# Making the low part of a weight block on GpSimd in four instructions of 256 columns in place of one of 1024

## The chip, the cores and the metric

The kernel runs on one core of one Trainium2 chip. The metric is the device time of one execution in microseconds (us), the median of several runs. TensorE is called PE in the profile, VectorE DVE, ScalarE ACT and GpSimd POOL.

## The reference

A two-layer network on 512 tokens of width 1024, all in float32. Layer 0 mixes tokens with a state-space block (`mamba2_mixer`), layer 1 with windowed attention. Both then run `peer_ffn`, a feed-forward part that picks experts, and `ple_add`, a gated addition. Cut to the part in which most of the time is spent:

```python
def peer_ffn(x, norm_g, q_w, sub_keys, u, v):
    h = rmsnorm(x, norm_g).reshape(T, D)
    q = (h @ q_w).reshape(T, PEER_HEADS, 2, PEER_HALF)
    s = jnp.einsum('thcd,ckd->thck', q, sub_keys)
    s1, i1 = lax.top_k(s[:, :, 0], PEER_TOPK)
    s2, i2 = lax.top_k(s[:, :, 1], PEER_TOPK)
    ...
    best_s, best_pos = lax.top_k(cand_s, PEER_TOPK)
    idx = jnp.take_along_axis(cand_i, best_pos, axis=-1)
    gate = jax.nn.softmax(best_s, axis=-1)
    a = jnp.einsum('nd,nhkd->nhk', hb, u[ib])
    w = gb * jax.nn.gelu(a, approximate=False)
    return jnp.einsum('nhk,nhkd->nd', w, v[ib])
```

The 16384 experts have a row in `u` and a row in `v`, each of 1024 numbers.

## The kernel before

**Products in three terms.** Each float32 operand of a large product is split into a high part (rounded to the type that TensorE takes fast) and a low part, the rest. `mm3` adds high by high, high weight by low data, and low weight by high data (lines L199, L200, L201). A weight block is 128 rows by 1024 columns and holds eight 128x128 tiles; a product over a block is 24 matmuls, three for each tile `k`.

**The split of a weight block.** `next_w` hands out the blocks in a fixed order. A block is loaded by a DMA into `wraw` (three buffers), ACT copies it into `whi` (L168), and then `lo_eng` writes `wlo = wraw - whi` (L169), one instruction of 1024 columns. `lo_eng` is GpSimd everywhere but in the loop over the `v` blocks, where it is DVE. The split runs two blocks ahead of the product that uses it (`SA = 2`). 391 blocks are split on GpSimd, 256 on DVE.

**The stages.** The state-space block, the query products, the gates and the attention work on 512 tokens. In `peer`, the first 128 tokens are done by gathering rows: GpSimd issues an indirect DMA for a row of `u` for each token (`row`, L692), DVE multiplies it with the token's vector, which lies in PSUM (`pair`, L675). The other 384 tokens are done densely: a loop over the 128 blocks of `u` ("the u loop"), then a loop over the 128 blocks of `v` ("the v loop"). Between the blocks of the u loop DVE works off a list of items (`bg`): the top-k search (L781 to L785, `cand` L800), the decoding of the positions (`eq` L828 to L838, `gk` L847), and for four tokens at a time a pair of one-hot tables, `early` (L877) and `og` (L879), which PE multiplies (`gmm`, L892). How many items come after a block is set by a credit (`BRATE`), and how many gathers by `URATE`.

**Order.** Nothing reorders the program: each engine runs its instructions in the order of the code, and semaphores make them wait. On GpSimd a gather therefore stands between two splits, and on PE a `gmm` between two blocks.

Of the kernel before, what the change touches and what calls it, by code (L numbers as in the profile page):

```python
# [11 lines left out]
F32 = _mybir.dt.float32  # L12
# [5 lines left out]
OP = _mybir.AluOpType  # L18
# [4 lines left out]
D = 1024  # L23
# [6 lines left out]
ND = NT - NG  # L30
NJ = HEADS * TOPK
LAG = 4
PAIR = (5, 6)
QT = 4
GSCALE = 32768.0
# [26 lines left out]
class Net:  # L62
    def __init__(self, ctx, tc, t):
# [3 lines left out]
        for i in range(8):  # L67
            if i not in PAIR:
                self.bank(i)
# [25 lines left out]
    def bank(self, i):  # L95
        return (self.psp if i in PAIR else self.psum).tile([P, 512], F32, name=f"bank{i}")

# [55 lines left out]
    def next_w(self):  # L153
        if self.wn is not None:
            w, self.wn = self.wn, None
            return w
        nc = self.nc
        i = self.nuse
        while self.ndma < min(len(self.srcs), i + self.LA + 1) or self.nsplit < min(len(self.srcs), i + self.SA + 1):
            if self.ndma < min(len(self.srcs), i + self.LA + 1) and self.ndma < self.nsplit + 3:  # L160
                self.ahead()
                continue
            if self.nsplit >= min(len(self.srcs), i + self.SA + 1):
                break
            r = self.split_q.pop(self.nsplit)
            hi = self.hl.tile([P, D], F32R, name="whi")
            lo = self.hl.tile([P, D], F32R, name="wlo")
            nc.scalar.activation(hi, r, AF.Copy)  # L168
            self.lo_eng.tensor_tensor(lo, r, hi.bitcast(F32), op=OP.subtract)  # L169
            self.split_q["w", self.nsplit] = (hi, lo)  # L170
            self.nsplit += 1
        self.nuse += 1
        return self.split_q.pop(("w", i))
# [463 lines left out]
    def peer(self, L):  # L637
# [28 lines left out]
        def gather_step():  # L666
            i = self.gi
            if i is None or i >= 2 * NJ + LAG:
                return
            self.gi += 1  # L670
            if i >= LAG:
                c, r = i - LAG, got.pop(i - LAG)
                j = c % NJ
                if c < NJ:
                    vt.scalar_tensor_tensor(r, r, 1.0, self.pair, op0=OP.mult, op1=OP.mult,  # L675
                                            accum_out=wg[:, 0, j:j + 1])
                    if j % 16 == 15:
                        js = slice(j - 15, j + 1)
                        vt.tensor_scalar(wg[:, 0, js], wg[:, 0, js], rv0, None, op0=OP.mult)
                        nc.scalar.activation(wg[:, 1, js], wg[:, 0, js], AF.Gelu)  # L680
                elif j == 0:
                    vt.tensor_scalar(yg, r, wg[:, 0, j:j + 1], None, op0=OP.mult)
                else:
                    vt.scalar_tensor_tensor(yg, r, wg[:, 0, j:j + 1], yg, op0=OP.mult, op1=OP.add)  # L684
            c = i - LAG - 8
            if c >= 0 and c % 16 == 15 and c < NJ:
                js = slice(c - 15, c + 1)
                vt.tensor_tensor(wg[:, 0, js], wg[:, 1, js], gate[:, js], op=OP.mult)
            if i < 2 * NJ:
                got[i] = rowt[i % len(rowt)]  # L690
                j = i % NJ
                nc.gpsimd.indirect_dma_start(  # L692
                    out=got[i], out_offset=None, in_=t["u"] if i < NJ else t["v"].rearrange("a p d -> (a p) d"),
                    in_offset=bass.IndirectOffsetOnAxis(ap=eg[:, j:j + 1], axis=0))
# [21 lines left out]
        def load_ga(j):  # L716
            if j < NBLK:
                gal[j] = gsz[0][:, j % 4, :ND]
                nc.sync.dma_start(gal[j], GA[j])
# [24 lines left out]
        with ExitStack() as ctx:  # L744
# [231 lines left out]
            for j in range(NBLK):  # L976
# [19 lines left out]
                if j >= NBLK - 3:  # L996
                    load_ga(j - NBLK + 3)
            while self.gi < NJ + LAG:
                gather_step()
        with vctx:  # L1000
# [6 lines left out]
            for j in range(NBLK):  # L1007
# [4 lines left out]
                if j == NBLK - VT:  # L1012
                    while self.gi < 2 * NJ + LAG:
                        gather_step()
# [536 lines left out]
```

## Time and profile before

| | |
|---|---|
| median of 3 runs | 3542.51 us (3539.78 to 3543.81) |
| profiled execution | 3534.58 us, of it 3532.8 us from the first to the last instruction |
| busy PE | 3377.5 us (96%) |
| busy DVE | 2808.9 us (80%) |
| busy GpSimd | 1676.7 us (47%) |
| busy ACT | 1453.3 us (41%) |

Busy time counts an instruction from its start to its end. If an instruction is held up after its start, that time is in it too, so a busy engine need not be a working one. PE is near full, and what a change can give is what PE stands idle. The u loops lie at about 650 to 1330 us (layer 0) and 2250 to 2930 us (layer 1).

### The profile page before, as it was taken

The numbers are of one execution on the slowest core, as the hardware profiler recorded it, in microseconds if no ns is written. First come the engines' busy times: TensorE is split into PE (matmuls) and PEld (weight loads), VectorE is DVE, ScalarE is ACT, GpSimd is POOL, SyncE is SP. The second block draws the span as 40 slices with busy tenths as digits, with TensorE's granted clock in tenths as the row PEclk, the third lists the DMA queues.
The fourth block names the chain that finished last, engine by engine and source line by source line (L and its number), as shares of the span: only waits on it lengthen the run. The fifth ranks groups of instructions, "written<-read, shape, count | busy, mean of one in ns | idle before, by whom it ended". The sixth has DMA issues, their size and how long they took to land.

```text
span 3532.8 us, 50923 instructions
## 1 busy us (share of the span) xinstructions
PE 3377.5 (96%) x18814; PEld 3107.8 (88%) x18814; DVE 2808.9 (80%) x4878; ACT 1453.3 (41%) x2198; POOL 1676.7 (47%) x995
## 2 busy tenths in 40 slices
PE   8999999989999999999998899989999999999997
PEld 5777777988999999999996667979999999999996
DVE  7677776899999857877777865899999848877775
ACT  4333333434444533333334553434444543333334
POOL 3333344566776684322215225566676685322213
PEclk9999999999999999999999999999999999999999
DMA  3222222478888899999983112478887899999992
GB/s 115 90 72 72 72 66 62 152 252 294 286 310 273 303 330 360 361 336 344 338 283 103 42 64 86 128 243 310 282 306 265 309 323 354 362 345 333 343 311 87
DMA packets 357290, 827.42 MB, mean 234 GB/s; under 512 B 30000, under 2 KB 196528, under 8 KB 350896
## 3 DMA queue, kind: packets, MB, share of 16 engines
q1 hardware_dynamic: 235136, 448.59, 39.6%
q0 software_dynamic: 73728, 268.47, 21.1%
q10 hardware_dynamic: 48176, 107.10, 7.8%
q8 instruction: 147, 2.41, 0.3%
q14 instruction: 103, 0.84, 0.1%
HBM read 717.09 MB, written 106.95 MB: 233 GB/s over the span
## 4 chain that ended last, share of the span: by engine, by line
PE 64%; DVE 27%; issue 4%; DMA 2%; POOL 2%; ACT 2%; DVEq 0%; SPq 0%; POOLq 0%; ACTq 0%
PE bank L199 19%; PE bank L200 19%; PE bank L201 19%; DVE row L675 4%; PE bank L892 3%; DVE og L879 3%; DVE early L877 2%; DVE eq L835 2%; DVE cand L800 1%; DVE eq L832 1%; POOL wlo L169 1%; POOL row L692 1%; PE bank L539 1%; DVE cu L483 1%; DMA gsz<-GA 1%
## 5 line engine op out<-in xcount | busy, mean ns | idle before, releaser
L169 POOL TENSOR_TENSOR wlo<-wraw,whi 128x1024 fp32r<-128x1024 f32 x391 | 966.9, 2475 | 850.0 <-ACT whi L168 803.5
L168 ACT ACTIVATE whi<-wraw 128x1024 fp32r<-128x1024 f32 x647 | 685.2, 1061 | 700.8 <-issue 329.9
L201 PE MATMUL bank<-hhi,wlo 128*128 128x384 f32 x2048 | 697.8, 341 | 19.9 <-POOL wlo L169 19.7
L199 PE MATMUL bank<-hhi,whi 128*128 128x384 f32 x2048 | 708.6, 346 | 0.0
L200 PE MATMUL bank<-hlo,whi 128*128 128x384 f32 x2048 | 696.3, 340 | 0.0
L200 PE MATMUL bank<-vlo,whi 128*128 128x384 f32 x2032 | 684.4, 337 | 2.9 <-DVE vlo L741 2.9
L199 PE MATMUL bank<-vhi,whi 128*128 128x384 f32 x2032 | 685.0, 337 | 0.2 <-ACT vhi L739 0.2
L201 PE MATMUL bank<-vhi,wlo 128*128 128x384 f32 x2032 | 683.8, 337 | 0.0
L692 POOL DMA_INDIRECT row<-v,eg x256 | 317.5, 1240 | 718.7 <-DVE yg L684 704.2
L169 DVE TENSOR_TENSOR wlo<-wraw,whi 128x1024 fp32r<-128x1024 f32 x256 | 313.4, 1224 | 152.7 <-ACT whi L168 151.8
L201 PEld LDWEIGHTS bank<-hhi,wlo 128*128 128x128 f32 x2048 | 388.2, 190 | 24.7 <-POOL wlo L169 24.6
L199 PEld LDWEIGHTS bank<-hhi,whi 128*128 128x128 f32 x2048 | 390.9, 191 | 0.0
L200 PEld LDWEIGHTS bank<-hlo,whi 128*128 128x128 f32 x2048 | 389.6, 190 | 0.0
L200 PEld LDWEIGHTS bank<-vlo,whi 128*128 128x128 f32 x2032 | 383.0, 188 | 4.8 <-DVE vlo L741 4.8
L199 PEld LDWEIGHTS bank<-vhi,whi 128*128 128x128 f32 x2032 | 383.0, 188 | 1.0 <-ACT vhi L739 0.5
L201 PEld LDWEIGHTS bank<-vhi,wlo 128*128 128x128 f32 x2032 | 383.0, 188 | 0.0
L675 DVE SCALAR_TENSOR_TENSOR row<-row,pair 128x1024 f32<-128x1024 f32 x256 | 305.4, 1213 | 70.3 <-DMA row<-u,eg 70.3
L684 DVE SCALAR_TENSOR_TENSOR yg<-row,wg,yg 128x1024 f32<-128x1024 f32 x254 | 348.6, 1372 | 13.8 <-DMA row<-v,eg 13.7
L987 ACT ACTIVATE ga<-bank 128x384 f32<-128x384 f32 x256 | 125.7, 491 | 514.2 <-PE bank L201 513.9
L692 POOL DMA_INDIRECT row<-u,eg x256 | 282.9, 1105 | 98.0 <-DVE row L675 48.7
L199 PE MATMUL bank<-z,whi 128*128 128x512 f32 x728 | 322.6, 443 | 6.2 <-DVE sg L1131 6.2
L200 PE MATMUL bank<-z,whi 128*128 128x512 f32 x728 | 292.1, 401 | 3.4 <-DVE z L259 3.4
(321 smaller groups left out, 5151.6 us busy)
## 6 DMA issues: line engine op xcount, KB each, us to landing
wraw<-ut SPq DMA_DIRECT2D x256, 512.0 KB, 4.6
wraw<-v SPq DMA_DIRECT2D x256, 512.0 KB, 6.1
wraw<-wlin SPq DMA_DIRECT2D x135, 512.0 KB, 3.5
GA<-ga ACTq DMA_DIRECT2D x256, 192.0 KB, 4.5
G<-gsz ACTq DMA_DIRECT2D x48, 1024.0 KB, 7.3
gv<-G SPq DMA_DIRECT2D x96, 512.0 KB, 9.5
gsz<-GA SPq DMA_DIRECT2D x256, 192.0 KB, 7.2
PJ<-nf ACTq DMA_DIRECT2D x16, 256.0 KB, 2.0
```

What stands on the lines that cost most here:

```text
L168: nc.scalar.activation(hi, r, AF.Copy)
L169: self.lo_eng.tensor_tensor(lo, r, hi.bitcast(F32), op=OP.subtract)
L199: mm(out, whi, xhi, start=start, stop=False)
L200: mm(out, whi, xlo, start=False, stop=False)
L201: mm(out, wlo, xhi, start=False, stop=stop)
L675: vt.scalar_tensor_tensor(r, r, 1.0, self.pair, op0=OP.mult, op1=OP.mult, accum_out=wg[:, 0, j:j + 1])
L684: vt.scalar_tensor_tensor(yg, r, wg[:, 0, j:j + 1], yg, op0=OP.mult, op1=OP.add)
L692: nc.gpsimd.indirect_dma_start(out=got[i], out_offset=None, in_=t["u"] if i < NJ else t["v"].rearrange("a p d -> (a p) d"), in_offset=bass ...
L835: vt.tensor_tensor(eq[:, :n], eq[:, :n], eq[:, n:2 * n], op=OP.add)
L879: vt.tensor_tensor(og, o[:, 0:1].to_broadcast([P, 2, P, QT]), gT[:, :, None, ts].to_broadcast([P, 2, P, QT]), op=OP.mult)
L892: mm(ps[:, q * P:(q + 1) * P], o[0][:, 1, :, q], o[1][:, j, :, q], start=(j == 0), stop=(j == 1))
L987: nc.scalar.activation(ga[:, NG:], ps[:, NG:], AF.Gelu)
```

## The change

The instruction on L169 is replaced by a loop. On GpSimd it writes 256 columns four times; on DVE it stays one of 1024 columns. Lines behind it move by up to three.

```diff
+LOP = 4
...
             nc.scalar.activation(hi, r, AF.Copy)
-            self.lo_eng.tensor_tensor(lo, r, hi.bitcast(F32), op=OP.subtract)
+            n = D if self.lo_eng is nc.vector else D // LOP
+            for q in range(0, D, n):
+                self.lo_eng.tensor_tensor(lo[:, q:q + n], r[:, q:q + n], hi.bitcast(F32)[:, q:q + n], op=OP.subtract)
```

GpSimd's queue in the u loop before (a `DMA` row is a gather; names in brackets are the semaphores that the row waits for):

```order
152 L692 DMA row_5517<-u,eg 128x1024 [waits DMASW3_49,DVE_49]
153 L169 TENSOR_TENSOR wlo<-wraw,whi 128x1024 [waits DMAHW4_49,PE_49,Activation_49]
154 L692 DMA row_5518<-u,eg 128x1024 [waits DMASW4_49,DVE_49]
155 L692 DMA row_5519<-u,eg 128x1024 [waits DMASW5_49,DVE_49]
156 L169 TENSOR_TENSOR wlo<-wraw,whi 128x1024 [waits DMAHW6_49,PE_49,Activation_49]
```

The same place in GpSimd's queue after the change:

```order
251 L695 DMA row_4687<-u,eg 128x1024 [waits DMASW2_49,DVE_49]
252 L172 TENSOR_TENSOR wlo<-wraw,whi 128x256 [waits DMAHW2_49,PE_49,Activation_49]
253 L172 TENSOR_TENSOR wlo<-wraw,whi 128x256 x3
254 L695 DMA row_5772<-u,eg 128x1024 [waits DMASW3_49,DVE_49]
```

Only the first of the four waits; the other three follow it at once, and the gathers stay where they were.

PE's queue at the start of a block of the u loop before (`hhi` and `hlo` are the two parts of the data):

```order
3737 L199 MATMUL bank_7464<-hhi_4710,whi 128x384 [waits Activation_49]
3738 L200 MATMUL bank_7464<-hlo_4711,whi 128x384
3739 L201 MATMUL bank_7464<-hhi_4710,wlo 128x384 [waits Pool_49]
3740 L199 MATMUL bank_7464<-hhi_4757,whi 128x384
3741 L200 MATMUL bank_7464<-hlo_4758,whi 128x384
3742 L201 MATMUL bank_7464<-hhi_4757,wlo 128x384
3743 L199 MATMUL bank_7464<-hhi_4840,whi 128x384
3744 L200 MATMUL bank_7464<-hlo_4841,whi 128x384
3745 L201 MATMUL bank_7464<-hhi_4840,wlo 128x384
```

The same place in PE's queue after the change:

```order
3739 L204 MATMUL bank_7833<-hhi_4926,wlo 128x384 [waits Pool_49]
3740 L202 MATMUL bank_7833<-hhi_4976,whi 128x384
3741 L203 MATMUL bank_7833<-hlo_4977,whi 128x384
3742 L204 MATMUL bank_7833<-hhi_4976,wlo 128x384
3743 L202 MATMUL bank_7833<-hhi_5062,whi 128x384
3744 L203 MATMUL bank_7833<-hlo_5063,whi 128x384
3745 L204 MATMUL bank_7833<-hhi_5062,wlo 128x384 [waits Pool_49]
```

PE now waits for GpSimd at every second tile, for a quarter each time, in place of once for the whole block. The order of the instructions on PE, DVE, ACT and the DMA queues is the same in both.

## Rows read from the trace of the kernel before

**Rows 1.** The page, section 1: busy time, share of the span, instructions

```profile
PE 3377.5 (96%) x18814; PEld 3107.8 (88%) x18814; DVE 2808.9 (80%) x4878; ACT 1453.3 (41%) x2198; POOL 1676.7 (47%) x995
```

**Rows 2.** Stretches: length, then busy PE, PEld, DVE, ACT, POOL, clock, DMA

```profile
650.00:1000.00 350.00, 324.46 (x1932) 315.37 (x1931) 330.65 (x666) 154.96 (x196) 233.81 (x133) 0.97 0.78 265
1000.00:1330.00 330.00, 321.20 (x1942) 313.32 (x1941) 261.26 (x358) 152.09 (x191) 244.15 (x138) 0.99 0.88 304
1500.00:1700.00 200.00, 200.00 (x1155) 200.00 (x1155) 158.87 (x191) 71.06 (x96) 45.39 (x45) 1.00 0.99 340
2250.00:2600.00 350.00, 324.93 (x1930) 316.12 (x1929) 329.95 (x673) 154.53 (x197) 233.00 (x132) 0.97 0.78 263
```

**Rows 3.** Waits of PE, 650 to 1000: total us, times, longest

```profile
PE bank L892 <- DVE og L879: 11.3, 6, 3.2
PE bank L201 <- POOL wlo L169: 9.4, 4, 7.3
PE bank L862 <- DVE gk L847: 4.6, 1, 4.6
```

**Rows 4.** GpSimd's time line just before the longest of these waits

```profile
717.02 0.95 POOL L692 DMA_INDIRECT row<-u,eg  x1 [7.21 <-DVE row L675]
```

**Rows 5.** DVE's time line in the u loop: start, length, instruction

```profile
785.11 2.92 DVE L879 TENSOR_TENSOR og<-early,gT 128x1024 f16<-128x1024 f16 x1
787.96 0.68 DVE L877 TENSOR_TENSOR early<-iota,iT 128x1024 f16<-128x1024 f16 x1
788.74 0.69 DVE L879 TENSOR_TENSOR og<-early,gT 128x1024 f16<-128x1024 f16 x1
```

**Rows 6.** GpSimd's time line in the same stretch

```profile
785.09 2.39 POOL L169 TENSOR_TENSOR wlo<-wraw,whi 128x1024 fp32r<-128x1024 f32 x1 [1.81 <-ACT whi L168]
787.63 1.23 POOL L692 DMA_INDIRECT row<-u,eg  x1
```

**Rows 7.** DVE's groups, 650 to 1330: count, busy us, mean ns, idle before

```profile
L675 DVE SCALAR_TENSOR_TENSOR row<-row,pair 128x1024 f32<-128x1024 f32 x128 | 152.7, 1214 | 33.6 <-DMA row<-u,eg 33.6
L877 DVE TENSOR_TENSOR early<-iota,iT 128x1024 f16<-128x1024 f16 x96 | 117.4, 1223 | 0.0
L879 DVE TENSOR_TENSOR og<-early,gT 128x1024 f16<-128x1024 f16 x96 | 105.7, 1101 | 36.6 <-PE bank L892 28.1
```

**Rows 8.** DVE's time line at the start of the kernel

```profile
15.40 2.85 DVE L259 SCALAR_TENSOR_TENSOR z<-x,cols,z 128x512 fp32r<-128x512 f32 x1
18.18 2.84 DVE L242 TENSOR_TENSOR acc<-acc,nf 128x512 f32<-128x512 f32 x1
20.94 2.82 DVE L259 SCALAR_TENSOR_TENSOR z<-x,cols,z 128x512 fp32r<-128x512 f32 x1
23.68 0.68 DVE L242 TENSOR_TENSOR acc<-acc,nf 128x512 f32<-128x512 f32 x1
24.29 0.74 DVE L259 SCALAR_TENSOR_TENSOR z<-x,cols,z 128x512 fp32r<-128x512 f32 x1
```

**Rows 9.** GpSimd's time line in the same stretch (x3: three merged)

```profile
15.18 8.03 POOL L169 TENSOR_TENSOR wlo<-wraw,whi 128x1024 fp32r<-128x1024 f32 x3 [0.85 <-ACT whi L168]
```

**Rows 10.** Line L169 on GpSimd in the whole run: shortest/median/longest ns

```profile
L169 POOL TENSOR_TENSOR wlo<-wraw,whi x391: 2344/2405/3421, 15.2 to 3497.9; 128x1024 fp32r<-128x1024 f32 x196
```

**Rows 11.** GpSimd's time line at the end: six of 256 columns, merged

```profile
3520.60 4.15 POOL L1194 TENSOR_TENSOR o<-x,rb 128x256 f32<-128x256 f32 x6 [8.68 <-ACT rb L1186]
```

**Rows 12.** GpSimd's groups, 650 to 1330

```profile
L169 POOL TENSOR_TENSOR wlo<-wraw,whi 128x1024 fp32r<-128x1024 f32 x128 | 318.2, 2487 | 154.3 <-ACT whi L168 152.7
L692 POOL DMA_INDIRECT row<-u,eg x128 | 141.5, 1105 | 49.2 <-DVE row L675 24.7 <-issue 7.5 <-DVE eg L853 4.8
```

**Rows 13.** Waits of PE, 0 to 50

```profile
PE bank L200 <- DVE z L259: 8.1, 6, 4.0
```

**Rows 14.** Waits of PE, 1860 to 1960 (gates of layer 0)

```profile
PE bank L199 <- DVE sg L1131: 6.2, 1, 6.2
PE bank L308 <- DVE rst L301: 3.5, 2, 2.9
```

## The prediction

> **What bounds the kernel now.** I read the page first: PE is busy 96% of the span, DVE 80%, GpSimd 47% [rows 1]. So a gain can only come out of what PE stands idle, and the next question was where. The stretches answer it. In the v loop PE is busy 200.00 of 200 us, and nothing changes there, since DVE makes the low parts. In the first half of the u loop PE lacks 350 - 324.5 = 25.5 us and in the second 330 - 321.2 = 8.8 us; layer 1 repeats the first with 25.1 [rows 2], and I take its second half as 8.8 too. DVE is busy 331 of the 350 us there, so DVE is what PE waits for. The list of PE's waits agrees: 11.3 us for `og` and 4.6 us for `gk`, both DVE's. The 9.4 us for `wlo` look like GpSimd's, but the longest, 7.3 us [rows 3], falls just after a gather in GpSimd's queue that had waited 7.21 us for DVE's `row`; the split stood behind it [rows 4]. All three waits come of DVE being late.
>
> The time lines then show why DVE is late. `og` started at 785.11, 20 ns after a split on GpSimd, and took 2.92 us; the next one took 0.69 [rows 5]. The split ran from 785.09 to 787.48 [rows 6], and `og` ended 0.55 us later. So it did nothing until the split was through, and that time counts as busy. The one-hot operations have two inputs in SBUF. L675 has one of its two in PSUM, and 128 of them average 1.21 us [rows 7]: no hold is to be seen in them.
>
> The Trainium skill ("SBUF — State Buffer", section "Who interferes with whom") says the same: a DVE instruction with two SBUF inputs and a GpSimd instruction share a port pair that one of them holds for its whole instruction, and the other blocks. By that rule a shorter GpSimd instruction means a shorter hold, and the trace agrees as far as one hold of 2.2 us goes.
>
> **What the change costs on GpSimd.** The trace has GpSimd operations of 256 columns: six in a row in 4.15 us, 0.69 each [rows 11]. A block in four is then 4 x 0.69 = 2.77 us, against a median of 2.405 [rows 10]; with no cost for an instruction at all it would stay at 2.405. I take the measured 2.77: 0.36 us more for a block, 391 x 0.36 = 141 us of GpSimd. What hides it: in the u loop GpSimd stands idle 154.3 us ahead of 128 splits, 1.21 us for each [rows 12]. Queued behind a split are the gathers (L692), and DVE's `row` waits for these; without the cover each microsecond would come back as a later block for PE.
>
> **What it moves on DVE.** The question is whether DVE gets in between two GpSimd instructions that follow at once. At the start of the kernel three splits run back to back, 8.03 us in all [rows 9], and three DVE operations start 2.77 us apart [rows 8]: one got in behind each split. Each such visit made GpSimd 2.77 - 2.40 = 0.37 us later. For a quarter and a DVE operation taking turns this gives 0.69 + 0.37 = 1.06 us, of which DVE's own share is 0.68, so a turn costs DVE 0.38 us. Now a hold is up to 2.2 us.
>
> In one u loop the one-hot operations lose 96 x (1.223 - 0.68) + 96 x (1.101 - 0.69) = 52 + 39 = 91 us [rows 5, 7]. A layer's block takes PE 645.7/128 = 5.04 us of work [rows 2], and 192/128 = 1.5 of these operations fall in it. GpSimd's block then takes about 2.77 + 1.5 x 0.37 = 3.3 us, two thirds of 5.04, so some two thirds of the 192 meet it and lose 0.38 each: 49 us. DVE gets back 42 us a layer; the bounds are 91 - 192 x 0.38 = 18 (all meet it) and 91 (none does). The top-k and decoding operations gain in the same way; I leave them out as a reserve.
>
> How much reaches PE: some half of the 42 us lies in the first 350 us, about as much as PE's 25.5 us of waiting there. I take 20 of 25.5, and 5 of 8.8 in the second half, where DVE has room already. That is 25 us a layer, 50 for two; the most is 2 x 34.3 = 69, and with DVE's relief at its lower bound I put 10 a layer, 20.
>
> **At the start** PE waits 8.1 us for `z` [rows 13]. Five DVE operations run there from 15.40 to 25.03 [rows 8], 9.6 us; at 1.06 each they take 5.3. Gain 4 us, of at most 8.
>
> **At the gates of layer 0** PE waits 9.7 us for two DVE results [rows 14]. With the share of the u loop (25 of 34.3) 7 us come back, of at most 9.7; the lower end is 3.
>
> **Waits that are added.** PE now waits at each second tile. The rows of the v loop show what a wait costs that is already over: each block there starts with waits for ACT and for DVE, and 1155 matmuls fill 200.00 us without a gap [rows 2]. I take 0. Where PE does wait for a block, the first quarter is there after 0.69 us in place of 2.4; that is part of the 25. DMA: `wraw` comes free with the fourth quarter, up to 1 us later, against a block's 5.04 us and three buffers; 0.
>
> **The sum.** 50 + 4 + 7 = 61 us. The profiled execution took 3534.6, so 3473.6; the median of the runs lies 7.9 above it. Predicted: 3542.5 - 61 = 3481.5 us.
>
> **The rivals.**
>
> *The hold is paid in instalments (0.15).* Where DVE has two-input operations one after the other, each meets the next quarter: four holds of 0.38 in place of one of 2.2. For it: the runs of `og` and `early` [rows 5]. Against it: 1.21 us of L675 stands between many of them, during which a quarter costs nothing. With 18 us of relief: 20 + 4 + 3 = 27 us, 3515.
>
> *GpSimd becomes late (0.09, slower).* A block costs GpSimd 2.77 + 1.105 for a gather + 0.15 between them [rows 6, 12] = 4.03 us, and each DVE operation that gets in adds 0.37. It decides from (5.04 - 4.03)/0.37 = 2.7 such visits a block on. Against it: 1.5 one-hot operations a block, which all together give 4.58. For it: where there is no `gmm`, PE's block is 24 x 0.173 = 4.16 us [rows 2], and with 1.17 gathers GpSimd needs 4.21; the lead of two blocks covers that for a while. With three visits a block: 0.10 x 256 = 26 us and no relief, 3568; with four, over 100 us.
>
> *The port is not given up between the quarters (0.06, slower).* Then DVE waits for the whole block as now, and the block is 2.77/2.40 = 1.15 times as long: 91 x 0.15 = 14 us more of DVE a layer, half of it on PE, 14 us for both: 3556. Against it: the start of the kernel, where DVE did get in [rows 8, 9]; but those splits each waited for ACT, and the new quarters wait for nothing. The Trainium skill speaks for this rival ("GPSIMD Engine Reference", section "2.1 Instruction dispatch"): one GpSimd instruction does not hold back the next, and a core begins it as soon as its own share is done. By that the pair might never be seen free; no row here shows a split with no wait of its own.
>
> *DVE's relief does not reach PE (0.06).* PE would meet the next wait at the same points, a DMA or ACT: 3542, no change.
>
> **How the numbers follow.** The forecast has 0.64, between 3456 (all idle time named above: 69 + 8 + 9.7 = 86 us) and 3505. The range reaches from 3456 to 3545: it takes in the instalments and no change, 0.85 in all, and leaves out the two slower cases. A measurement of this kernel can tell some 0.2%, 7 us. Faster by more: 0.64 + 0.15 + a little of the rest, 0.81; the same 0.05; slower 0.14.
>
> **What would show it.** Right: 1564 GpSimd instructions of 256 columns; `early` and `og` averaging some 0.95 us in place of 1.16, their longest under 1.2; PE's idle time in 350 us of the u loop down to some 5 us; GpSimd's busy time up by 141 us and more, since its waits for DVE count as busy. Wrong: `og` still at 2.9 us beside a run of quarters (the port is kept); PE's waits for `wlo` grown in number (GpSimd is late); holds short and PE's waits for `og` and `gk` as before (something else binds).

## The result, and the profile after

The changed kernel takes 3495.3 us (median of four runs, 3490.6 to 3499.8) against 3542.4 before (3539.8 to 3543.8): a ratio of 0.9869, 95% interval 0.9853 to 0.9885, so 47 us or 1.3% faster. The prediction was 3481.5 with 3456 to 3545. The profiled execution took 3494.4 us, 0.9 below its median, where that of before lay 7.9 below; so the two profiles differ by some 40 us only, and the stages below add up to that.

In the changed kernel every line number from the split on is 3 higher. The page's busy times, share of the span and instructions, to set beside [rows 1]:

```profile
PE 3374.0 (97%) x18814; PEld 3109.2 (89%) x18814; DVE 2647.7 (76%) x4878; ACT 1454.1 (42%) x2198; POOL 1941.5 (56%) x2168
```

DVE does the same 4878 instructions in 161 us less, and GpSimd spends 265 us more. The split alone takes 295 us more (966.9 before, 1262.3 now): 141 were forecast for the four instructions themselves, and the rest are quarters that were held up (0.84 us on average against a median of 0.74). The stretches, to set beside [rows 2] (length, then busy PE, PEld, DVE, ACT, POOL, clock, DMA; the last but one is the v loop):

```profile
650.00:1000.00 350.00, 339.25 (x2034) 332.60 (x2033) 315.44 (x673) 162.27 (x204) 301.69 (x348) 0.99 0.83 286
1000.00:1330.00 330.00, 315.69 (x1886) 306.35 (x1884) 215.03 (x321) 145.52 (x184) 264.07 (x302) 0.98 0.87 303
1330.00:1530.00 200.00, 199.88 (x1153) 199.88 (x1154) 163.74 (x199) 77.00 (x101) 65.85 (x48) 1.00 1.01 355
2200.00:2550.00 350.00, 340.85 (x2018) 331.72 (x2017) 316.99 (x754) 159.80 (x211) 292.95 (x339) 0.99 0.78 267
```

PE's idle time fell from 25.5 to 10.75 us in the first 350 us of the u loop, and rose from 8.8 to 14.3 in the next 330. What PE waits for, first in 650 to 1000 [rows 3], then in 1000 to 1330 (us in total, times, longest):

```profile
PE bank L895 <- DVE og L882: 9.0, 5, 3.4
PE bank L204 <- POOL wlo L172: 1.8, 1, 1.8
...
PE bank L204 <- POOL wlo L172: 6.0, 8, 2.1
PE bank L895 <- DVE og L882: 4.6, 3, 3.2
PE bank L203 <- DVE vlo L744: 2.7, 2, 1.4
```

For the kernel before, what PE waits for in 1000 to 1330:

```profile
PE bank L892 <- DVE og L879: 4.4, 5, 1.4
PE bank L862 <- DVE gk L847: 3.6, 1, 3.6
PE bank L201 <- POOL wlo L169: 0.7, 2, 0.4
```

Two things should strike the reader. A wait for `og` of 3.4 us is longer than any of before, although no piece of a split is longer than 1.8 us now. And in the second stretch there are eight waits for GpSimd's `wlo`, 6.0 us, in place of two of 0.7. DVE's groups from 650 to 1330 [rows 7]:

```profile
L678 DVE SCALAR_TENSOR_TENSOR row<-row,pair 128x1024 f32<-128x1024 f32 x128 | 152.8, 1212 | 50.5 <-DMA row<-u,eg 50.5
L880 DVE TENSOR_TENSOR early<-iota,iT 128x1024 f16<-128x1024 f16 x96 | 110.8, 1154 | 0.0
L882 DVE TENSOR_TENSOR og<-early,gT 128x1024 f16<-128x1024 f16 x96 | 87.4, 910 | 57.6 <-PE bank L895 49.6 <-DVE early L880 0.9
```

`og` fell from 1.10 to 0.91 us, but `early` from 1.22 to 1.15 only. The first row shows a price: DVE waits 50.5 us for gathered rows where it waited 33.6.

**By stage.** From the first matmul of each stage to that of the next, in the two traces, us saved: start to the first interleaved work 4.1; rest of layer 0's state-space part 7.8; u loops 12.0 and 15.4; v loops -2.0 and -3.9; gates of layer 0 4.7; all others together 2.2. The sum is 40.3. Each figure is a difference of two single traces. The v loops of the kernel with quarters outside the u loops alone (in the table below) also took 1.5 and 0.5 us longer than before, so the -2.0 of layer 0 is not clear of what traces differ by.

**The pass-overs.** At the kernel's start DVE and GpSimd take turns as forecast. DVE's time line there, to set beside [rows 8]:

```profile
15.63 0.74 DVE L262 SCALAR_TENSOR_TENSOR z<-x,cols,z 128x512 fp32r<-128x512 f32 x1
16.29 1.22 DVE L245 TENSOR_TENSOR acc<-acc,nf 128x512 f32<-128x512 f32 x1
17.43 1.21 DVE L262 SCALAR_TENSOR_TENSOR z<-x,cols,z 128x512 fp32r<-128x512 f32 x1
18.57 1.21 DVE L245 TENSOR_TENSOR acc<-acc,nf 128x512 f32<-128x512 f32 x1
19.70 1.21 DVE L262 SCALAR_TENSOR_TENSOR z<-x,cols,z 128x512 fp32r<-128x512 f32 x1
```

In the u loop that is not always so. First GpSimd's time line, then DVE's in the same stretch (x4: the four quarters of a block, merged):

```profile
789.75 1.08 POOL L695 DMA_INDIRECT row<-u,eg  x1 [0.30 <-DVE og L882]
790.85 2.82 POOL L172 TENSOR_TENSOR wlo<-wraw,whi 128x256 fp32r<-128x256 f32 x4
793.82 1.22 POOL L695 DMA_INDIRECT row<-u,eg  x1 [0.16 <-issue]
795.06 2.81 POOL L172 TENSOR_TENSOR wlo<-wraw,whi 128x256 fp32r<-128x256 f32 x4
```

```profile
791.86 2.36 DVE L880 TENSOR_TENSOR early<-iota,iT 128x1024 f16<-128x1024 f16 x1
794.33 0.69 DVE L882 TENSOR_TENSOR og<-early,gT 128x1024 f16<-128x1024 f16 x1
794.94 3.50 DVE L880 TENSOR_TENSOR early<-iota,iT 128x1024 f16<-128x1024 f16 x1
```

`early` at 791.86 arrives in the second quarter and ends at 794.22, 0.55 us after the block's end at 793.67. Two quarter ends went by without it. The next one arrives at 794.94 behind a gather and gets in when the whole block is through. I call this a pass-over. To count them I took the DVE operations that were held by over 0.12 us, had arrived in the first three quarters, and met a quarter that had not itself been delayed. Of those, in both u loops, that met a block which began less than 0.1 us behind a gather, 17 of 52 were passed over; where GpSimd had paused before the block, none of 40. Not in this count are operations that began up to 0.2 us before such a block, like the second one above: all 17 of these that were held had to wait for the whole block.

### The profile page after: what moved, and what is told of

Read it like the earlier page. It is cut to its first block, busy times and chain, and to the rows that moved or that the text cites. A ratio compares the mean times of both kernels' runs of the same rounds, so it can differ in the third digit from the quotient of the medians.

```text
span 3492.6 us, 52247 instructions
## 1 busy us (share of the span) xinstructions
PE 3374.0 (97%) x18814; PEld 3109.2 (89%) x18814; DVE 2647.7 (76%) x4878; ACT 1454.1 (42%) x2198; POOL 1941.5 (56%) x2168
## 3 DMA queue, kind: packets, MB, share of 16 engines
q8 instruction: 147, 2.41, 0.3%
## 4 chain that ended last, share of the span: by engine, by line
PE 70%; DVE 18%; POOL 5%; DMA 3%; issue 3%; ACT 1%; SPq 0%; POOLq 0%; ACTq 0%; DVEq 0%
PE bank L202 20%; PE bank L203 20%; PE bank L204 20%; PE bank L895 4%; POOL wlo L172 3%; DVE row L678 2%; DMA row<-u,eg 2%; DVE eq L838 1%; DVE og L882 1%; DVE early L880 1%; POOL row L695 1%; PE bank L968 1%; DVE eq L835 1%; PE bank L542 1%; DVE eq L831 1%
## 5 line engine op out<-in xcount | busy, mean ns | idle before, releaser
L172 POOL TENSOR_TENSOR wlo<-wraw,whi 128x256 fp32r<-128x256 f32 x1564 | 1262.3, 839 | 601.0 <-ACT whi L169 553.0
L169 ACT ACTIVATE whi<-wraw 128x1024 fp32r<-128x1024 f32 x647 | 685.3, 1061 | 760.3 <-issue 303.5
L695 POOL DMA_INDIRECT row<-v,eg x256 | 294.2, 1149 | 733.5 <-DVE yg L687 719.0
L687 DVE SCALAR_TENSOR_TENSOR yg<-row,wg,yg 128x1024 f32<-128x1024 f32 x254 | 327.9, 1291 | 38.0 <-DMA row<-v,eg 38.0
L695 POOL DMA_INDIRECT row<-u,eg x256 | 276.1, 1079 | 49.6 <-issue 23.4
```

The lines of the kernel that those rows point to most:

```text
L172: self.lo_eng.tensor_tensor(lo[:, q:q + n], r[:, q:q + n], hi.bitcast(F32)[:, q:q + n], op=OP.subtract)
L695: nc.gpsimd.indirect_dma_start(out=got[i], out_offset=None, in_=t["u"] if i < NJ else t["v"].rearrange("a p d -> (a p) d"), in_offset=bass ...
```

## The experiments

Ratios are to the kernel before, run on the same chip. "DVE's loss" in a u loop is the sum, over all DVE instructions from the loop's first matmul to the v loop's, of what each took above the 5th percentile of its kind in the traces compared. The main numbers of all kernels, layer 0 / layer 1, in us:

| kernel | ratio (95% interval) | DVE's loss in u loop | u loop | v loop |
|---|---|---|---|---|
| before | 1 | 181 / 174 | 677.6 / 676.9 | 535.5 / 537.8 |
| changed, four quarters | 0.9869 (0.9853 to 0.9885) | 112 / 115 | 665.6 / 661.5 | 537.5 / 541.7 |
| no low part in u loops | 0.9753 (0.9738 to 0.9768) | 12 / 12 | 644.4 / 643.2 | 534.1 / 535.2 |
| quarters in reverse | 0.9886 (0.9871 to 0.9901) | 113 / 117 | 664.9 / 663.4 | 535.9 / 539.3 |
| quarters in u loops alone | 0.9933 (0.9919 to 0.9946) | 115 / 115 | 668.0 / 661.2 | 536.3 / 540.1 |
| quarters outside u loops | 0.9964 (0.9950 to 0.9977) | 179 / 179 | 681.0 / 676.2 | 537.0 / 538.3 |
| halves | 0.9962 (0.9948 to 0.9975) | 140 / 143 | 670.5 / 673.6 | 537.1 / 538.1 |
| eighths | 1.0067 (1.0047 to 1.0087) | 154 / 156 | 703.2 / 695.6 | 542.8 / 543.9 |
| memset behind gathers | 0.9889 (0.9871 to 0.9908) | 123 / 124 | 666.2 / 658.4 | 547.1 / 546.1 |
| plain transfers | 0.9814 (0.9798 to 0.9831) | 98 / 101 | 656.8 / 658.3 | 536.1 / 540.8 |
| quarters, three waits | 0.9864 (0.9844 to 0.9885) | 91 / 92 | 662.2 / 658.8 | 539.5 / 542.2 |
| quarters, one wait | 0.9820 (0.9802 to 0.9837) | 85 / 86 | 654.7 / 650.7 | 539.8 / 543.0 |
| halves, one wait | 0.9922 (0.9904 to 0.9939) | 121 / 119 | 671.5 / 668.1 | 536.5 / 539.8 |
| one wait, DVE at loop's end | 0.9734 (0.9716 to 0.9752) | 82 / 89 | 645.1 / 644.2 | 533.8 / 534.9 |

**How much was there to gain.** In the u loops GpSimd's quarters are left out and the high part stands in for the low one:

```
             u = 82 <= self.nsplit < 210 or 383 <= self.nsplit < 511
-            for q in range(0, D, n):
+            for q in range(0, 0 if u else D, n):
...
-            self.split_q["w", self.nsplit] = (hi, lo)
+            self.split_q["w", self.nsplit] = (hi, hi if u else lo)
```

> The changed kernel without any low part in the two u loops: GpSimd's four instructions are left out there and PE multiplies by the high part a second time (so the output lacks the low parts' share); PE's work is the same in count and size, and DVE meets no GpSimd arithmetic in the u loops. Theory A: this is the most that shorter holds can give: PE's idle time in a u loop of about 32 us before (677.6 against 645.7) falls to under 8, the u loops take 650 us each, and the whole 3455 to 3470 us. If DVE's own work or DMA keeps PE waiting, the u loops stay at 660 and the whole at 3480 to 3495: then the 25 us a layer of the prediction were never to be had.

It took 3450.2 us. PE's first 350 us of the u loop, in the columns of [rows 2]:

```profile
650.00:1000.00 350.00, 350.00 (x2125) 344.47 (x2124) 259.32 (x704) 168.34 (x212) 79.92 (x79) 1.00 0.85 302
```

PE is never idle there, so neither DVE's own work nor a transfer bounds this stretch once GpSimd's arithmetic is gone. The u loops fall by 33 us each. That this is nearly the 34.3 us of idle time in the prediction is a coincidence: in layer 0 PE's idle time fell from 34.3 to 8.9 us (one wait, at 1208, for a weight block that landed late), and its busy time fell by 7.8 us besides. A part of these 7.8 is the clock: TensorE's granted clock was at 1.2 GHz, the lower of its two levels, for 27.3 us of this loop before, PE being busy in 16.8 of them, each time within or right behind waits of PE of 3 to 7 us. Here it is 10.2 us, with PE busy in 4.5. The change got 12.0 and 15.4 of the 33. The question for all other runs is who holds the rest.

**Which of the two effects: DVE let in, or PE let go early.** The quarters written last to first:

```
-            for q in range(0, D, n):
+            for q in range(D - n, -1, -n):
```

> The changed kernel with the four quarters of a block written from the last column to the first, so that PE's first tile waits for the quarter that is made last, as in one instruction of 1024; DVE meets quarters of the same size. Theory A (the gain is DVE let in between quarters): nearly all of the 47 us stays, 3493 to 3508 us, since only the few blocks for which PE waits at once come up to 2.2 us later; og and early keep their means (0.91 and 1.15 us). Rival B (the gain is that PE may begin a block after its first quarter): it goes, 3530 to 3545 us.

3498.0 us, a ratio of 0.9886. PE's first tile waits for the last quarter here, and the two intervals overlap; rival B falls. DVE's loss is the same too (113 against 112). PE's waits in layer 0's u loop shift, for `wlo` to 12.5 us from 7.8 and for `og` to 7.6 from 13.6; whether being let go early is worth a few us cannot be told from these times.

**Where the gain arises.** Quarters in the u loops alone, and everywhere else:

```
-            n = D if self.lo_eng is nc.vector else D // LOP
+            n = D if self.lo_eng is nc.vector or not (82 <= self.nsplit < 210 or 383 <= self.nsplit < 511) else D // LOP
```

> Four instructions for the blocks of the two u loops alone, one of 1024 columns for all others. Theory A: the u loops gave 12.0 and 15.4 us of the change by the two profiles, so 3515 us (3510 to 3522); the v loops still lose their 2 and 4 us, since what they begin with is left by the u loops. Rival C (GpSimd becoming late in the u loops eats their gain, and the time of the change came from elsewhere): 3530 to 3545.

> Four instructions everywhere but in the two u loops. Theory A: the state-space part of layer 0 gave 11.9 us by the two profiles and the gates of layer 0 4.7, with 2 to 4 more in small stages, so 3522 us (3516 to 3528), and the v loops lose nothing. If the parts add up, this gain and that of the u loops alone make 47 us together. Rival (the predicted 4 us at the start and 7 at the gates, nothing more): 3531.

3512.5 and 3525.1 us: 0.67% and 0.36%, together 1.03% where the whole change gave 1.31%. With intervals of about 0.13% either way on each, I read from it that both parts carry gain, the u loops the larger; whether they add up exactly stays open. With quarters outside the u loops the state-space part took 566.4 us (572.2 before, 564.4 in the changed kernel) and the gates 53.6 (58.3 before, 53.6), so most of the 7.8 and all of the 4.7 us there come from quarters in those stages; with quarters in the u loops alone they took 573.4 and 58.2.

**More or fewer pieces.** `LOP = 2` and `LOP = 8`:

> Two instructions of 512 columns in place of four of 256. If what a DVE operation loses is the rest of the instruction that it meets, a hold is up to 1.2 us (mean 0.6) in place of 0.65 (mean 0.35), and GpSimd's block costs 0.2 us less: the u loops give about two thirds of what four gave, 3512 us (3503 to 3520). If GpSimd's lateness (its waits for the turns, more of them with more pieces) is what keeps four from giving all, halves are as good or better: 3490 to 3500.

> Eight instructions of 128 columns. A block costs GpSimd some 8 x 0.38 = 3.1 us without any turn, and up to eight turns a block. Theory A with turns as the remaining price: DVE's holds fall to 0.3 us, but GpSimd becomes late and PE's waits for wlo pass 30 us a layer; 3500 to 3530 us, worse than four. If short holds still pay more than GpSimd's time costs: 3480 to 3490.

Halves gave 14.6 us and eighths cost 23.6, so four is the best of the three. Halves took 3528.8, longer than either theory had said. A hold often does not end with the instruction that DVE meets: 26 of 59 operations behind a gather were passed over. But the one-hot operations lose less in halves (58 us in a u loop) than in quarters (67); it is the other operations that lose more, about 82 against 45 in layer 0. So the one-hot operations alone do not set what PE gets, and why the others lose so much more in halves stays open. Eighths took 3567.0, above the range of both theories, and not as either had said: PE waits 30.7 us for `og` in layer 0's u loop and 14.9 for `wlo`, where 30 had been expected for `wlo`. DVE's loss did not fall below that of quarters, it rose to 154. `early` and GpSimd's split from 650 to 1330:

```profile
L880 DVE TENSOR_TENSOR early<-iota,iT 128x1024 f16<-128x1024 f16 x96 | 131.8, 1373 | 0.0
...
L172 POOL TENSOR_TENSOR wlo<-wraw,whi 128x128 fp32r<-128x128 f32 x983 | 477.6, 521 | 39.5 <-ACT whi L169 37.7
```

`early` is slower than before the change (1.223 us), beside instructions of 0.52 us on average: 51 of the 59 operations that met a block straight behind a gather were passed over. A pause also came less often, since GpSimd has only 39.5 us of idle time left ahead of its splits, against 154.3 for the kernel before [rows 12]. So the length of a GpSimd instruction alone does not decide the hold.

**What a pass-over hangs on.** If the gather leaves GpSimd in a state that arithmetic ends, a memset behind it should help; if the indirect gather alone does it, a plain transfer of as many bytes should not.

```
+                nc.gpsimd.memset(tick, 0.0)
```

> The changed kernel with a GpSimd memset of 16 columns behind every gather. In the three traces with quarters in the u loop 45 of 156 DVE operations that met a block begun straight behind a gather were passed over until the block's end (1.3 to 2.7 us), and none of some 110 where the block came after a pause or after arithmetic. Theory D (the gather leaves GpSimd in a state in which its next instructions run on without a free moment): with arithmetic between, no more pass-overs, longest early and og under 1.5 us, PE's wait for og (9.0 us in 350) under 4, the whole 3480 to 3488 us. Rival (it is how close the block follows, or chance): as many pass-overs as before, 3493 to 3500, a little later for the memsets.

```
-                nc.gpsimd.indirect_dma_start(
-                    out=got[i], out_offset=None, in_=t["u"] if i < NJ else t["v"].rearrange("a p d -> (a p) d"),
-                    in_offset=bass.IndirectOffsetOnAxis(ap=eg[:, j:j + 1], axis=0))
+                nc.gpsimd.dma_start(got[i], t["ut" if i < NJ else "v"][L * NBLK + j])
```

> The changed kernel with each gathered row replaced by a plain transfer of 128 whole rows from a fixed place, issued by GpSimd at the same point of its queue with the same buffers (so the output is made from wrong rows; bytes are the same). Theory D: if it is the indirect gather's work on GpSimd that leaves it out of step, no pass-overs here, and GpSimd has the gather's time free too (1.1 us each), so 3470 to 3485 us. Rival: the pass-overs stay, since any DMA issued by GpSimd does it: 3490 to 3500.

Theory D falls by both. Behind the memsets 24 of 68 were passed over, the same third. (3505.8 us is above both ranges. The v loops of that profile are 9.6 and 4.4 us longer than in the changed kernel with no wait that accounts for it; I did not find why, and its total says nothing on D.) Behind plain transfers with no pause 11 of 20 were passed over, and behind a pause none of 61. The plain kernel's 3478.2 us lie in theory D's range all the same, but not for D's reason: GpSimd spends 0.56 us on a transfer in place of 1.08 and pauses more often (151 us of idle time ahead of its splits against 71), and behind a pause nothing is passed over. That this is the whole of its gain is not shown. What is common is a GpSimd that has worked on without a pause since it issued a transfer.

**The wait for completion.** In the changed kernel three quarters of a block wait for nothing. All 1173 quarters that follow another begin before the one ahead has ended by the trace, by 0.04 us in the median. Here each of them waits on the semaphore of the one before (then, only the second):

```
-                self.lo_eng.tensor_tensor(lo[:, q:q + n], r[:, q:q + n], hi.bitcast(F32)[:, q:q + n], op=OP.subtract)
+                ins = self.lo_eng.tensor_tensor(lo[:, q:q + n], r[:, q:q + n], hi.bitcast(F32)[:, q:q + n], op=OP.subtract).ins
+                if q and n < D:
+                    self.tc.add_manual_dep(ins, prev.name, _mybir.DependencyInfo(_mybir.DependencyClass.Sync, _mybir.DependencyReason.DATA), reason="done")
+                prev = ins
```

> The changed kernel in which each quarter also waits on the semaphore of the quarter before it, so that it begins only when all of GpSimd has finished that one; the memsets behind the gathers did not end the pass-overs (24 of 68 behind them, as 45 of 156 before). Theory E (behind a gather without a pause, parts of GpSimd begin the next quarter while others still work on the last, so the port is never seen free; a pause or a wait for completion ends that): no DVE operation passed over, longest early and og under 1.5 us, one-hot loss per u loop down from 67 us to some 50. DVE gains 17 us a layer; by the runs so far PE gets back about a fifth of what DVE gets back, 3 to 4 us a layer, less what the waits cost GpSimd (three a block): 3485 to 3495 us. Rival (the pass-overs have another cause): they stay at a third, and the waits only cost: 3495 to 3510.

> As the one with a wait at each quarter, but only the second quarter waits for the first. Theory E: if one wait sets GpSimd's parts in step and they stay so to the block's end, only DVE operations that arrive in the first quarter may still be passed over, and by one quarter at most; 3484 to 3493 us, since GpSimd pays one wait in place of three. Rival (parts fall out of step again in each quarter): pass-overs from the second quarter on as many as without, 3493 to 3500.

> Two instructions of 512 columns, the second waiting for the first to be completed. Without the wait halves gave 14 us; 26 of 59 DVE operations that met a block straight behind a gather were passed over. Theory E: no pass-overs, DVE's loss per u loop from 140 us to about 120, and by a fifth of that 4 us of PE a layer: 3515 to 3522 us. Rival (the size of the hold alone matters): no change from halves, 3525 to 3532.

No DVE operation was passed over any more: none of 109 behind a gather with three waits, none of 68 with one (and of those that began just before the block, none of 17 and none of 18). In halves, of the operations that arrived in the first half of a block straight behind a gather, 26 of 36 were passed over without the wait and none of 36 with it. The kernel with one wait, DVE's groups from 650 to 1330, then DVE's time line and GpSimd's:

```profile
L885 DVE TENSOR_TENSOR og<-early,gT 128x1024 f16<-128x1024 f16 x96 | 89.2, 929 | 64.4 <-PE bank L898 55.7 <-PE bank L207 1.9 <-DVE early L883 0.5
L883 DVE TENSOR_TENSOR early<-iota,iT 128x1024 f16<-128x1024 f16 x96 | 86.6, 902 | 0.0
```

```profile
791.35 1.09 DVE L883 TENSOR_TENSOR early<-iota,iT 128x1024 f16<-128x1024 f16 x1
792.55 1.05 DVE L885 TENSOR_TENSOR og<-early,gT 128x1024 f16<-128x1024 f16 x1
793.52 1.22 DVE L883 TENSOR_TENSOR early<-iota,iT 128x1024 f16<-128x1024 f16 x1
```

```profile
789.23 1.08 POOL L698 DMA_INDIRECT row<-u,eg  x1 [0.30 <-issue]
790.32 3.87 POOL L172 TENSOR_TENSOR wlo<-wraw,whi 128x256 fp32r<-128x256 f32 x4
```

Here too the block starts straight behind a gather. Two DVE operations get in between its quarters, and the third, which arrives in the last quarter, right behind it. One wait gave 3476.8 us, 1.8% under the kernel before, and halves with a wait 3512.3 (the interval lies clear of that without). Theory E holds for the waits: a wait for completion ends the pass-overs, and one at the second quarter is enough to the end of the block. Both times with one wait were better than expected: of DVE's 27 us PE got back 11 in a u loop, more than a fifth. Three waits gave 3490.7: an undisturbed block takes GpSimd at least 2.75 us without a wait, 2.92 with one and 3.16 with three, and PE's waits for `wlo` from 650 to 1300 come to 10.0 us with three against 6.0 with one.

What goes on inside GpSimd no trace shows. The Trainium skill ("GPSIMD Engine Reference", section "2.1 Instruction dispatch") says that a GpSimd instruction does not hold back the next, that each core begins it when its own share is done while others may still be writing, and that a wait on the completion semaphore is what to put between two instructions that need the order. The runs fit that: quarters that begin before the last one has ended, and 0 of 177 pass-overs with waits against 17 of 52 without. They do not show it. Overlap by the trace alone does not make a pass-over: behind a pause the quarters overlap by the same 0.04 us, and so do the third and fourth quarter in the kernel with one wait, and nothing is passed over there. And a quarter that waits begins 0.08 us behind the one ahead; whether the completion or just this gap is what helps, no run separates.

**The end of the u loop.** A part of what was left stood at the loop's end. Busy times of its last 70 us in layer 0, for the kernel before, the changed one and the one with one wait (columns as in [rows 2]):

```profile
1255.00:1325.00 70.00, 69.29 (x392) 68.65 (x391) 39.99 (x32) 25.04 (x34) 61.23 (x35) 1.00 0.95 329
```

```profile
1231.00:1301.00 70.00, 63.60 (x344) 60.55 (x344) 24.32 (x27) 24.35 (x33) 64.95 (x75) 0.98 0.84 291
```

```profile
1221.00:1291.00 70.00, 65.24 (x363) 62.55 (x362) 23.74 (x29) 24.42 (x33) 62.38 (x73) 1.00 0.89 300
```

Before, PE lacked 0.7 us there; in the changed kernel it lacks 6.4 (layer 1: 0.7 and 5.0), GpSimd is busy 65 of 70 us and DVE 24. The last `gmm` has run by then, at 1211. So the last 12 blocks' low parts go to DVE, whole:

```
+            eng = nc.vector if 198 <= self.nsplit < 210 or 499 <= self.nsplit < 511 else self.lo_eng
+            n = D if eng is nc.vector else D // LOP
```

> The kernel with one wait in a block (3476.8 us), and in the last 12 blocks of each u loop DVE makes the low part in one instruction, as it does in the v loop; DVE is busy there 17 of 50 us, GpSimd 47 of 50. The rival of the prediction (GpSimd becomes late where a block has no gmm) would be true for this place: PE's 5 us of waiting for wlo between 1250 and 1300 us go, in both layers, and the v loop begins on time: 3462 to 3470 us. If the wait there is for weights or rows that arrive late (DMA), or DVE's low part stands in its queue behind a row that has not arrived, nothing is gained: 3474 to 3485 us.

```profile
1212.00:1282.00 70.00, 70.00 (x403) 70.00 (x402) 39.28 (x47) 26.08 (x35) 34.55 (x38) 1.00 0.99 356
```

3448.9 us, 2.7% under the kernel before. PE is busy all of the 70 us (69.1 in layer 1). The v loops gain 6 and 8 us as well, which I had not put into the expectation: GpSimd's lateness had been carried into them. In layer 0 PE waited 3.9 us for `vlo` and 2.4 for `wlo` from 1280 to 1830 with one wait, and 0.2 and nothing here. The u loops are at 645.1 and 644.2, close to the 644.4 and 643.2 without low parts, of which 8.9 in layer 0 are the late weight block. This version leaves nothing out and beats both kernels.

## Why the prediction was right, and where its terms were off

The mechanism was right: DVE is let in between shorter instructions, and PE waits less for it. That the time came within 14 us of the forecast is in part luck, since terms that were too high and terms that were too low or left out partly cancel.

**GpSimd's price (2.77 us a block): right.** The shortest block takes 2.75.

**The turns (1.06 us each): right but for size.** They follow 1.14 us apart at the start, and five DVE operations took 5.28 us where 5.3 was forecast. The gain at the start was 4.1 against 4.

**DVE's loss in the one-hot operations (91 us falling to 49): the step that failed first.** It fell from 91.6 to 66.7. The forecast had every operation let in at the next quarter's end. A third of those behind a gather are not, and a pass-over costs up to 2.8 us in place of 0.38. Of the 192 operations 75 were held for 0.39 us on average, as forecast for one turn, and 15 for 2.4 us: these 15 make 36.5 of the 66.7 us. With one wait none is held that long and the loss is 44.4, near the forecast, so the relief of 25 us in place of 42 comes of the pass-overs and not of the instalments of the first rival, by which all 192 would be held. So the mechanism of the prediction is what happens when pass-overs are taken away, and the rival "the port is not given up between the quarters" was true for a part of the blocks. The top-k and decoding operations that I had left as a reserve gave another 45 us, so that DVE's relief was 70 us in layer 0 and not 42.

**How much reaches PE (25 us a layer): too high, 12.0 and 15.4.** I had let DVE's relief count almost whole as long as PE waits. By the table the u loops give back between a tenth and some two fifths of what DVE's loss falls by, and with eighths they grew longer although it fell. So there is no fixed rate; the 33 us for 169 when all of it goes are no rate either, since PE had hardly more to get. What the traces show beside it is that 38 of DVE's 70 us went into waiting, for rows (50.5 us in place of 33.6) or for PE (`og` 49.6 in place of 28.1, [rows 7]). That this is the reason is a reading; no run tests it.

**The rival "GpSimd becomes late": true at the end of the u loops.** I had seen the place (4.21 us of GpSimd against a block of 4.16) and said that the lead of two blocks covers it for a while. The loop's last 70 us cost 5.7 and 4.3 us more than before, and the v loops, which I had put at nothing, 2.0 and 3.9: 16 us together. In the rest of the u loops the change gave 17.7 and 19.7 (12.0 + 5.7, 15.4 + 4.3).

**The gates (7) gave 4.7; the state-space part, not in the sum, gave 7.8.** DVE's loss there fell from 69 to 43 us; I had looked for PE's waits at the start and not behind it.

**The added waits of PE at nothing: as far as tested, right.** With the order reversed, where the first tile waits for the last quarter, PE's queue has 128 waits for GpSimd in a u loop in place of 512, and the time is not shorter.

Step by step, by the profiles: 61 forecast, less 12.6 in the u loops before their end, 10.0 at their end, 5.9 in the v loops and 2.3 at the gates, and 7.8 + 2.2 + 0.1 more elsewhere, is 40.3.

## What to carry to other kernels

When two engines share a port, cutting one engine's long instructions helps the other fully only if it is let in between the pieces: here pieces that waited for nothing kept a third of the operations behind a gather waiting past a piece's end, and one wait for completion behind the first piece was worth some 17 us here, over a third of what the whole change gave. After such a cut look at the places where the engine that now works longer was already nearly full, above all at the end of a loop, and give the work there to an engine that stands idle. Read the gain from what the waiting engine gets back, not from what the relieved one does.

## What the runs showed of the hardware

- An operation that waits for the shared port is not always next: behind a gather without a pause 17 of 52 were passed over at one or more instruction ends in the changed kernel, and 51 of 59 with pieces of 128 columns; behind a pause none of 40. A wait for completion (0.17 us a block for one) ended it.
- A memset of 16 columns (0.13 us) between the gather and the block changed nothing: 24 of 68 passed over.
- GpSimd's subtraction costs 2.41, 1.30, 0.74 and 0.46 us for 1024, 512, 256 and 128 columns (medians of the whole runs); by these four about 0.18 us of each does not depend on the columns, an estimate.
